# Six instead of four groups a layer by Strassen's scheme, with the differences' buffers moved and one product 512 wide

## The chip, the cores and the metric

The kernel runs on one core of a Trainium2 chip. The metric is the device time of one execution in microseconds. Before the change it is 1974.23 us, the median of three runs (1973.96 to 1975.21). TensorE (PE) multiplies, VectorE (DVE), ScalarE (ACT) and GpSimd (POOL) do the elementwise work, SyncE (SP) issues the transfers of weights.

## The reference, cut to what matters

```python
D_MODEL, SEQ, DEPTH = 2048, 256, 2
D_FF = 5632

def swiglu_ffn(x, g, w_in, w_out):
    h = rms_norm(x, g)
    gate, up = jnp.split(h @ w_in, 2, axis=-1)
    return x + (jax.nn.silu(gate) * up) @ w_out

def reference(...):
    for layer in range(DEPTH):
        if layer < N_REC:                      # layer 0: recurrent block (RG-LRU)
            x = recurrent_block(x, ...)
        else:                                  # layer 1: windowed attention with sinks
            ...
            x = attn_block(x, ..., k_band, v_band)
        x = swiglu_ffn(x, norm2_g[layer], ffn_w_in[layer], ffn_w_out[layer])
    return x
```

All of it is float32. The change touches the product `h @ w_in` of the two FFNs: 256 tokens, 2048 features in, 2 x 5632 out.

## The kernel before

**Tiles and passes.** The activations are kept transposed, features on partitions, 256 tokens (`T`) along the row. A weight chunk is a 128 x 1024 tile: 256 features in (two k tiles) by 512 out. It comes by one transfer into one of four `raw` tiles and is split into a high part (`hi`, on ACT, L306) and the rest (`lo`, on DVE, L309), both in a reduced float type that PE takes in one pass. An activation tile is split in the same way into a slot, 256 columns high, 256 low. A product is then three passes: high by high, high by low, low by high. In an ordinary chunk the weights are the stationary operand (in the ring `hi`/`lo`) and the activations move (in a slot): 2 k tiles x 4 blocks of outputs x 3 = 24 passes of 256 columns, all recorded at L375. Where a block has a whole bank of PSUM, the pair high by (high, low) can be one pass of 512 columns; `RUNS` and `SYNC` put three of these in a row at some places. Groups that are `paired` have two banks for four blocks and use none of them.

**Groups.** 512 columns of `w_in` by all 2048 features is a group: 8 chunks, 192 passes. An FFN has 22. In `ffn` the first `NS` of them go by Strassen's scheme: a chunk is a 2 x 2 product of blocks, done with seven products instead of eight, 21 passes a chunk, which is here called a turn (L476). In a turn the activations are the stationary operand (in slots, or sums of them, `forms`, also in slots) and 256 columns of weights move: either the ring's (`b<-hi,s`, `b<-lo,s`) or differences of the chunk's blocks (`b<-s,s`). The differences are computed by POOL from `raw` (L279 to L281, in `sums`) two sets in turn, and split by ACT (L289) and DVE (L291, in `split_sums`) into slots that `sums` takes from the same pool as all others. At a group's end `fast` adds the four banks into two slots `U` and `V` on DVE; four transposes on PE (L383, L386) turn the finished product back.

**Order.** All chunks are one list, `jobs`. `ffn` puts `AHEAD` = 8 ordinary chunks, then each turn followed by `OWN` = 2 ordinary chunks, then the remaining ordinary ones, then the groups of `w_out` (`project`). `stream` loads a chunk four jobs ahead, splits it three ahead and its differences two ahead. Everything else (norms, gates, split of hidden features: `later`) are background tasks that `run_bg` puts between, as far as a running estimate of DVE and ACT work allows. A task that finds no free slot or bank is asked again later; `need` runs tasks at once where a product must have their result.

**Slots and where they lie.** Slots are tiles of 2 KB a partition, `s0` to `s57`, and are made at their first use, after the other tiles. Tiles are placed in the order in which they are made. The `x`, `raw`, `hi` and `lo` tiles start 96 bytes past a multiple of 128 bytes; two tiles `rstd` of 1032 bytes shift what is made after them, so that all 58 slots start at 32 past such a multiple.

Of the kernel before, what the change touches and what calls it, by code (L numbers as in the profile page):

```python
# [12 lines left out]
F32 = mybir.dt.float32  # L13
F32R = mybir.dt.float32r
# [3 lines left out]
P = 128  # L18
# [31 lines left out]
class Trunk:  # L50
# [15 lines left out]
    DVE_TICK = 640.0  # L66
    ACT_TICK = 800.0

    NS = 4
    AHEAD = 8  # L70
    OWN = 2
    LS = 2
# [2 lines left out]
    def __init__(self, ctx, tc, dram):  # L75
        self.tc, self.nc, self.d = tc, tc.nc, dram
        nc = self.nc
        const = ctx.enter_context(tc.tile_pool(name="const", bufs=1))
        psum = ctx.enter_context(tc.tile_pool(name="psum", bufs=1, space=bass.MemoryType.PSUM))
        tmp = ctx.enter_context(tc.tile_pool(name="tmp", bufs=1))  # L80
        self.tmp = tmp
        self.par = const.tile([P, NPAR], F32, name="par")
        self.con = const.tile([P, NCON], F32, name="con")
        self.cc = const.tile([P, 32], F32, name="cc")
        self.x = [const.tile([P, 4, T], F32, name=f"x{i}") for i in range(4)]
        self.slots = deque(range(58))
        self.spool = const
        self.held = {}
        self.raw = [const.tile([P, 1024], F32, name=f"raw{i}") for i in range(4)]
        self.hi = [const.tile([P, 1024], F32R, name=f"hi{i}") for i in range(4)]  # L90
        self.lo = [const.tile([P, 1024], F32R, name=f"lo{i}") for i in range(4)]
        self.banks = deque(psum.tile([P, 512], F32, name=f"b{i}") for i in range(8))
        self.misc = 0
        self.started = False
        self.xin = 0
        self.other = None
        self.summing = False
        self.opening = None
# [12 lines left out]
        self.dve = 0.0  # L111
        self.act = 0.0
# [34 lines left out]
        self.nc.vector.reciprocal(out, a)  # L147


    def slot(self, dt=F32R):  # L150
        i = self.slots.popleft()
        s = self.spool.tile([P, 2 * T], dt, tag=f"s{i}", name=f"s{i}")
        self.held[id(s)] = (i, s)
        return s

    def free(self, s):
        self.slots.append(self.held.pop(id(s))[0])

    def half(self):
        if self.halves:  # L160
            return self.halves.popleft()
        s = self.slot(F32)
        h = s[:, 0:T]
        self.held[id(h)] = (s, h)
        return h
# [103 lines left out]
    def sums(self, i):  # L269

        raw, tt = self.raw[i % 4], self.nc.gpsimd.tensor_tensor
        if not self.sets:
            self.sets = deque([self.slot(F32), self.slot(F32)] + [self.slot() for _ in range(4)] for _ in range(2))
        s = self.sets.popleft()
        self.sets.append(s)
        self.jobs[i][2]["set"] = s
        b = raw[:, :].rearrange("p (b t) -> p b t", b=4)
        two = lambda q: q.rearrange("p (b t) -> p b t", b=2)
        tt(two(s[0][:, :]), b[:, 0:3:2, :], b[:, 1::-1, :], ALU.subtract)  # L279
        tt(s[1][:, 0:T], raw[:, 2 * T:3 * T], s[0][:, 0:T], ALU.subtract)  # L280
        tt(s[1][:, T:2 * T], raw[:, 3 * T:4 * T], s[1][:, 0:T], ALU.subtract)  # L281

    def split_sums(self, i):

        if len(self.jobs[i]) > 2:
            s = self.jobs[i][2]["set"]
            for z, a, b in ((s[0], s[2], s[3]), (s[1], s[4], s[5])):
                with self.tc.issue_after(self.behind[0]):
                    self.nc.scalar.activation(a, z, AF.Copy)  # L289
                with self.tc.issue_after(self.behind[1]):  # L290
                    self.nc.vector.tensor_tensor(b, z, a.bitcast(F32), ALU.subtract)  # L291
            self.dve += 1400
            self.act += 1200
# [152 lines left out]
    def strassen(self, src, xs, forms, done, last, left):  # L446

        st = {}
        jobs = []
        for c in range(ND // 2):  # L450
            part = {}

            def mm(hi, lo, c=c, part=part):
                if c == 0:
                    st["ps"] = [self.bank() for _ in range(4)]
                    st["begun"] = set()
                ps = st["ps"]
# [6 lines left out]
                t1, t3, t2, t4 = (tuple(s[n + q][:, h * T:h * T + T] for q in (0, 1)) for n in (2, 4) for h in range(2))  # L464
                todo = [(0, 0, A(0, 0), B(1)), (1, 1, A(1, 0), B(3)), (1, 0, S(1), t2), (2, 0, S(0), t1),
                        (2, 1, S(2), t3), (3, 0, S(3), B(2)), (3, 1, A(1, 1), t4)]
                if 0 < c < ND // 2 - 1:
                    todo = [todo[q] for q in (0, 1, 5, 3, 4, 2, 6)]
                if self.other is not None:
                    self.runs = self.RUNS  # L470
                    self.other = None
                for n, (b, h, w, m) in enumerate(todo):
                    if n == 4:
                        self.half_tick()
                    for i, j in ((0, 0), (0, 1), (1, 0)):
                        self.nc.tensor.matmul(ps[b][:, h * T:h * T + T], w[i], m[j], start=b not in st["begun"],  # L476
                                              stop=c == ND // 2 - 1 and i == 1, skip_group_check=True)
                        st["begun"].add(b)
                        self.since += 1
                left[0] -= 1  # L480
                if last and c == ND // 2 - 1:
                    for q in self.sets:
                        for t in q:
                            self.free(t)
                    self.sets = None
                if last:
                    for q in (fh, fl):
                        self.free(q)
                if c == ND // 2 - 1:
                    done(ps)  # L490
            jobs.append((src(c), mm, part))
        return jobs
# [64 lines left out]

    def prep_tile(self, k, gains):

        self.gained(k, gains)  # L560
        yield
        yield from self.squares(k)
# [91 lines left out]
    def ffn(self, l, xs, forms, r, gains, rn, out=None):  # L654
# [6 lines left out]
        def later(g, s):  # L661
            while left[0]:
                yield 1
            for h in range(2):
                while len(self.slots) < 2:
                    yield 1
                q = self.slot()
                self.split_act(q, s[:, h * T:h * T + T])
                hid[2 * g + h].ap = q
                hid[2 * g + h].ready = True  # L670
                yield
            self.free(s)

        for g in range(self.NS):
            def fast(ps, g=g):
                c1, U, V = self.t(), self.slot(F32), self.slot(F32)
                two = lambda q: q.rearrange("p (b t) -> p b t", b=2)
                twice = lambda q: q.unsqueeze(1).broadcast_to([P, 2, T])
                self.a(c1, ps[0][:, 0:T])
                self.tt(two(U[:, :]), two(ps[1][:, :]), twice(c1[:, :]), ALU.add)  # L680
                self.tt(two(V[:, :]), two(ps[2][:, :]), twice(U[:, 0:T]), ALU.add)
                self.tt(U[:, 0:T], ps[2][:, 0:T], V[:, T:2 * T], ALU.add)
                self.tt(V, ps[3], V, ALU.add)
                for b in ps:
                    self.free_bank(b)

                def task():
# [26 lines left out]
        for g in range(self.NS, NH // 2):  # L714
            def done(ps, g=g):
# [4 lines left out]
                def task():  # L720
# [3 lines left out]
                    for h in range(2):  # L724
# [648 lines left out]
```

## Time and profile before

| | |
|---|---|
| median of the runs | 1974.23 us |
| the profiled execution | 1976.51 us, of which the span is 1974.7 us |
| granted TensorE clock | 1.00 |
| Strassen stage, layer 0 | 317 to 568 us |
| Strassen stage, layer 1 | 1278 to 1529 us |
| PE's waits for other engines, in all | 4.9 us |

The span is what the instructions take, from the first to the last. A mean duration of one pass (282 ns for L375) holds its latency; passes overlap, and what counts is the distance from start to start. The chain in order of time gives it: a piece's length divided by its passes.

### The profile page before, as it was taken

The numbers are of one execution on the slowest core, as the hardware profiler recorded it, in microseconds if no ns is written. First come the engines' busy times: TensorE is split into PE (matmuls) and PEld (weight loads), VectorE is DVE, ScalarE is ACT, GpSimd is POOL, SyncE is SP. The second block draws the span as 40 slices with busy tenths as digits, with TensorE's granted clock in tenths as the row PEclk, the third lists the DMA queues.
The fourth block names the chain that finished last, engine by engine and source line by source line (L and its number), as shares of the span: only waits on it lengthen the run. The fifth ranks groups of instructions, "written<-read, shape, count | busy, mean of one in ns | idle before, by whom it ended". The sixth has DMA issues, their size and how long they took to land.

```text
span 1974.7 us, 40978 instructions
## 1 busy us (share of the span) xinstructions
PE 1966.7 (100%) x16762; PEld 1934.6 (98%) x16762; DVE 1428.8 (72%) x2073; ACT 1121.2 (57%) x1746; POOL 383.4 (19%) x356
## 2 busy tenths in 40 slices
PE   9999999999999999999999999999999999999999
PEld 9999999999999999999999889999999999999999
DVE  8988978988986655545668767888889665554443
ACT  6798766555555444434556776655556554444442
POOL 0000125555520000000002454354444000000000
PEclk9999999999999999999999999999999999999999
DMA  8555665665555555555555434565555656556664
GB/s 276 187 190 177 200 209 193 187 208 197 192 201 191 195 193 192 193 193 196 195 185 182 129 129 152 191 214 193 193 193 201 194 193 193 194 196 205 206 205 127
DMA packets 106204, 377.16 MB, mean 191 GB/s; under 512 B 11936, under 2 KB 14368, under 8 KB 106016
## 3 DMA queue, kind: packets, MB, share of 16 engines
q1 hardware_dynamic: 105408, 373.88, 57.7%
q8 instruction: 131, 2.15, 0.4%
q10 hardware_dynamic: 608, 0.66, 0.1%
q14 instruction: 57, 0.47, 0.1%
HBM read 371.88 MB, written 2.10 MB: 189 GB/s over the span
## 4 chain that ended last, share of the span: by engine, by line
PE 96%; DVE 2%; ACT 1%; issue 0%; POOL 0%; DMA 0%; ACTq 0%; DVEq 0%; POOLq 0%
PE b L375 84%; PE b L476 8%; PE b L386 1%; PE b L866 1%; PE b L383 1%; ACT s L123 1%; DVE lo L309 1%; PE b L1052 1%; ACT hi L306 0%; DVE s L1120 0%; DVE s L132 0%; DMA x<-in_x 0%; PE b L1061 0%; PE b L1062 0%; PE b L1063 0%
## 5 line engine op out<-in xcount | busy, mean ns | idle before, releaser
L375 PE MATMUL b<-s,hi 128*128 128x256 f32 (+1 forms) x9536 | 1301.0, 282 | 1.6 <-ACT s L123 1.0
L375 PEld LDWEIGHTS b<-s,hi 128*128 128x128 f32 x9536 | 1203.1, 188 | 21.4 <-ACT s L123 1.7
L309 DVE TENSOR_TENSOR lo<-raw,hi 128x1024 fp32r<-128x1024 f32 (+1 forms) x643 | 812.5, 1266 | 447.4 <-ACT hi L306 444.8
L306 ACT ACTIVATE hi<-raw 128x1024 fp32r<-128x1024 f32 (+1 forms) x643 | 676.0, 1054 | 588.6 <-PE b L375 508.1
L375 PE MATMUL b<-s,lo 128*128 128x256 f32 x4992 | 748.3, 277 | 0.0
L375 PEld LDWEIGHTS b<-s,lo 128*128 128x128 f32 x4992 | 651.0, 188 | 0.5
L279 POOL TENSOR_TENSOR s<-raw 128x512 f32<-128x512 f32 x64 | 120.8, 1888 | 233.3 <-DMA raw<-in_ffn_in 185.6
L291 DVE TENSOR_TENSOR s<-s,s 128x512 fp32r<-128x512 f32 x128 | 141.5, 1141 | 0.6 <-ACT s L289 0.3
L1142 POOL TENSOR_TENSOR s<-s 128x128 f32<-128x128 f32 x32 | 14.7, 462 | 537.0 <-ACT s L123 534.3
L476 PE MATMUL b<-s,s 128*128 128x256 f32 x768 | 105.6, 282 | 0.5 <-DVE s L291 0.5
L299 ACT ACTIVATE hi<-raw 128x768 fp32r<-128x768 f32 x64 | 54.1, 845 | 78.8 <-PE b L375 56.5
L476 PEld LDWEIGHTS b<-s,s 128*128 128x128 f32 x768 | 97.3, 189 | 0.8 <-DVE s L291 0.7
L123 ACT ACTIVATE s<-s 128x256 fp32r<-128x256 f32 (+3 forms) x180 | 69.1, 429 | 33.4 <-POOL s L508 19.5
L132 DVE TENSOR_TENSOR s<-s,s 128x256 fp32r<-128x256 f32 (+3 forms) x148 | 70.6, 509 | 19.8 <-ACT s L123 19.7
L476 PE MATMUL b<-hi,s 128*128 128x256 f32 x384 | 80.7, 281 | 0.0
L280 POOL TENSOR_TENSOR s<-raw,s 128x256 f32<-128x256 f32 x64 | 78.7, 1230 | 5.0
L300 DVE TENSOR_TENSOR lo<-raw,hi 128x768 fp32r<-128x768 f32 x64 | 70.5, 1102 | 12.6 <-PE b L375 8.1
L289 ACT ACTIVATE s<-s 128x512 fp32r<-128x512 f32 x128 | 73.6, 617 | 7.8 <-POOL s L281 7.8
L506 POOL TENSOR_TENSOR s<-s 128x128 f32<-128x128 f32 x16 | 14.0, 877 | 328.8 <-ACT s L123 328.8
L281 POOL TENSOR_TENSOR s<-raw,s 128x256 f32<-128x256 f32 x64 | 70.9, 1108 | 5.0
L476 PEld LDWEIGHTS b<-hi,s 128*128 128x128 f32 x384 | 64.6, 189 | 0.0
L123 ACT ACTIVATE s<-x,par 128x256 fp32r<-128x256 f32 (+1 forms) x112 | 52.6, 498 | 19.9 <-DVE x L132 13.5
(121 smaller groups left out, 1127.4 us busy)
## 6 DMA issues: line engine op xcount, KB each, us to landing
raw<-in_ffn_in SPq DMA_DIRECT2D x352, 512.0 KB, 3.5
raw<-in_ffn_out SPq DMA_DIRECT2D x176, 512.0 KB, 3.4
raw<-in_lru_in SPq DMA_DIRECT2D x62, 512.0 KB, 3.6
raw<-in_lru_out SPq DMA_DIRECT2D x32, 512.0 KB, 3.8
raw<-in_w_q SPq DMA_DIRECT2D x32, 512.0 KB, 3.4
raw<-in_w_o SPq DMA_DIRECT2D x32, 512.0 KB, 3.3
raw<-in_gate SPq DMA_DIRECT2D x8, 512.0 KB, 3.7
raw<-in_kv SPq DMA_DIRECT2D x8, 512.0 KB, 3.4
```

What stands on the lines that cost most here:

```text
L123: self.nc.scalar.activation(out, in_, func, **kw)
L132: self.nc.vector.tensor_tensor(out, a, b, op)
L279: tt(two(s[0][:, :]), b[:, 0:3:2, :], b[:, 1::-1, :], ALU.subtract)
L280: tt(s[1][:, 0:T], raw[:, 2 * T:3 * T], s[0][:, 0:T], ALU.subtract)
L281: tt(s[1][:, T:2 * T], raw[:, 3 * T:4 * T], s[1][:, 0:T], ALU.subtract)
L289: self.nc.scalar.activation(a, z, AF.Copy)
L291: self.nc.vector.tensor_tensor(b, z, a.bitcast(F32), ALU.subtract)
L300: low = self.nc.vector.tensor_tensor(lo[:, q], raw[:, q], hi[:, q].bitcast(F32), ALU.subtract)
L306: high = self.ins(self.nc.scalar.activation(hi[:, q], raw[:, q], AF.Copy))
L309: low = self.nc.vector.tensor_tensor(lo[:, q], raw[:, q], hi[:, q].bitcast(F32), ALU.subtract)
L375: self.nc.tensor.matmul(*args, **kw)
L476: self.nc.tensor.matmul(ps[b][:, h * T:h * T + T], w[i], m[j], start=b not in st["begun"], stop=c == ND // 2 - 1 and i == 1, skip_group_ch ...
```

## The change

`NS` is 6 instead of 4. Of the slots, `s57` to `s64` are now made right behind `lo`, ahead of the `rstd` tiles, and form a pool of their own (`odd`); `sums` puts the split differences there, and other F32 slots use it when it is free. The second pair of differences is split in two halves, so that high and low part of one difference stand side by side in a slot. The turn starts with the product of the fourth difference: its high by (high, low) is one pass of 512 columns into a whole bank (L484), and the low by high another; the other six products share the other three banks. `fast` adds the additional half bank. The scratch for dynamic DMAs is cut from its 16 KB to 2 KB a partition, where the additional slots go. Some tasks wait for more free slots.

```diff
-    NS = 4
+    NS = 6
...
-        self.slots = deque(range(58))
+        self.slots = deque(range(57))
+        self.odd = deque(range(57, 65))
...
+        for i in self.odd:
+            self.spool.tile([P, 2 * T], F32R, tag=f"s{i}", name=f"s{i}")
...
-    def slot(self, dt=F32R):
-        i = self.slots.popleft()
+    def slot(self, dt=F32R, odd=None):
+        odd = bool(self.odd) and dt == F32 if odd is None else odd
+        i = (self.odd if odd else self.slots).popleft()
...
-            self.sets = deque([self.slot(F32), self.slot(F32)] + [self.slot() for _ in range(4)] for _ in range(2))
+            self.sets = deque([self.slot(F32, False) for _ in range(2)] + [self.slot(F32R, True) for _ in range(4)]
+                              for _ in range(2))
...
-            for z, a, b in ((s[0], s[2], s[3]), (s[1], s[4], s[5])):
+            for z, a, b in ((s[0], s[2], s[3]), (s[1][:, 0:T], s[4][:, 0:T], s[4][:, T:2 * T]),
+                            (s[1][:, T:2 * T], s[5][:, 0:T], s[5][:, T:2 * T])):
...
-                todo = [(0, 0, A(0, 0), B(1)), (1, 1, A(1, 0), B(3)), (1, 0, S(1), t2), (2, 0, S(0), t1),
-                        (2, 1, S(2), t3), (3, 0, S(3), B(2)), (3, 1, A(1, 1), t4)]
+                t1, t3 = (tuple(s[2 + q][:, h * T:h * T + T] for q in (0, 1)) for h in range(2))
+                t2, t4 = (tuple(q[:, h * T:h * T + T] for h in range(2)) for q in s[4:6])
+                todo = [(0, 0, A(1, 1), t4), (3, 1, A(0, 0), B(1)), (1, 0, S(1), t2), (1, 1, A(1, 0), B(3)),
+                        (2, 0, S(0), t1), (2, 1, S(2), t3), (3, 0, S(3), B(2))]
                 if 0 < c < ND // 2 - 1:
-                    todo = [todo[q] for q in (0, 1, 5, 3, 4, 2, 6)]
+                    todo = [todo[q] for q in (0, 1, 3, 6, 4, 5, 2)]
...
-                    for i, j in ((0, 0), (0, 1), (1, 0)):
+                    if n == 0:
+                        self.nc.tensor.matmul(ps[b], w[0], s[5], start=b not in st["begun"],
+                                              stop=c == ND // 2 - 1, skip_group_check=True)
+                        st["begun"].add(b)
+                    for i, j in ((0, 0), (0, 1), (1, 0))[2 * (n == 0):]:
...
@@ prep_tile @@
+        while len(self.slots) < 3:
+            yield 1
...
@@ later @@
-                while len(self.slots) < 2:
+                while len(self.slots) < 4:
...
-                self.a(c1, ps[0][:, 0:T])
+                self.a(c1, ps[3][:, T:2 * T])
...
-                self.tt(V, ps[3], V, ALU.add)
+                self.tt(V[:, 0:T], ps[3][:, 0:T], V[:, 0:T], ALU.add)
+                self.tt(V[:, T:2 * T], ps[0][:, 0:T], V[:, T:2 * T], ALU.add)
+                self.tt(V[:, T:2 * T], V[:, T:2 * T], c4, ALU.add)
...
-                        if both is not None or h == 0 and left[0]:
+                        if both is not None or h == 0 and (left[0] or len(self.slots) < 8):
...
-    nc = bacc.Bacc("TRN2", target_bir_lowering=False, num_devices=1)
+    nc = bacc.Bacc("TRN2", target_bir_lowering=False, num_devices=1, dynamic_dma_scratch_size=2048)
```

Two places show how the instructions stand. The first is PE in a turn in the middle of a group of layer 0; a row is line, operation, output, moving operand, stationary operand and size. Before, from the third product on; `s44` and `s45` are differences, `s34` and `s51` a chunk's forms:

```order
L476 MATMUL b5_88<-hi2_77,s34_3334 128x256
L476 MATMUL b5_88<-lo2_81,s34_3334 128x256
L476 MATMUL b5_88<-hi2_77,s51_3335 128x256
L476 MATMUL b4_87<-s44_3869,s34_3334 128x256
L476 MATMUL b4_87<-s45_3870,s34_3334 128x256
L476 MATMUL b4_87<-s44_3869,s51_3335 128x256
```

After, from the head of the turn; `s57`, `s59` and `s60` are differences, `s33` and `s32` activations, `s1` and `s49` forms:

```order
L484 MATMUL b2_93<-s60_3880,s33_3233 128x512
L488 MATMUL b2_93<-s60_3880,s33_3233 128x256
L488 MATMUL b5_96<-hi2_77,s32_3219 128x256
L488 MATMUL b5_96<-lo2_81,s32_3219 128x256
L488 MATMUL b5_96<-hi2_77,s32_3219 128x256
L488 MATMUL b3_94<-hi2_77,s33_3233 128x256
L488 MATMUL b3_94<-lo2_81,s33_3233 128x256
L488 MATMUL b3_94<-hi2_77,s33_3233 128x256
L488 MATMUL b5_96<-hi2_77,s1_3342 128x256
L488 MATMUL b5_96<-lo2_81,s1_3342 128x256
L488 MATMUL b5_96<-hi2_77,s49_3343 128x256
L488 MATMUL b4_95<-s57_3877,s1_3342 128x256
```

The product of a difference that closed the turn now opens it, with a pass of 512 columns, and the differences come from slots 57 and up.

The second place is DVE at the end of the first Strassen group of layer 0, where the ring's splits (L309 and L300), the splits of differences (L291) and the group's sums (L132, from banks `b`) stand in one queue. Before:

```order
L291 TENSOR_TENSOR s57_3876<-s52_3873,s31_3875 128x512
L291 TENSOR_TENSOR s40_3878<-s53_3874,s55_3877 128x512
L309 TENSOR_TENSOR lo3_82<-raw3_74,hi3_78 128x1024
L300 TENSOR_TENSOR lo0_79<-raw0_71,hi0_75 128x768
L132 TENSOR_TENSOR s56_4643<-b3_86,t1_92 128x512
L132 TENSOR_TENSOR s35_4644<-b4_87,s56_4643 128x512
L132 TENSOR_TENSOR s56_4643<-b4_87,s35_4644 128x256
L132 TENSOR_TENSOR s35_4644<-b5_88,s35_4644 128x512
```

After (L316 and L307 are the ring's splits, L298 those of differences, L135 the sums):

```order
L135 TENSOR_TENSOR s45_4659<-b3_94,t1_100 128x512
L135 TENSOR_TENSOR s46_4660<-b4_95,s45_4659 128x512
L316 TENSOR_TENSOR lo1_80<-raw1_72,hi1_76 128x1024
L135 TENSOR_TENSOR s45_4659<-b4_95,s46_4660 128x256
L135 TENSOR_TENSOR s46_4660<-b5_96,s46_4660 128x256
L135 TENSOR_TENSOR s46_4660<-b2_93,s46_4660 128x256
L298 TENSOR_TENSOR s59_3878<-s15_3875,s57_3877 128x512
L135 TENSOR_TENSOR s46_4660<-s46_4660,t2_101 128x256
L298 TENSOR_TENSOR s58_3879<-s19_3876,s58_3879 128x256
L298 TENSOR_TENSOR s60_3880<-s19_3876,s60_3880 128x256
```

The sums are six instead of four, with a ring split and a split of differences between them, and a set of differences is split by three instructions instead of two.

More of the change, by code (lines that the diff above doesn't have):

```diff
@@ L156, in free @@
     def free(self, s):
-        self.slots.append(self.held.pop(id(s))[0])
+        i = self.held.pop(id(s))[0]
+        (self.slots if i < 57 else self.odd).append(i)
     def half(self):
@@ L161, in half @@
             return self.halves.popleft()
-        s = self.slot(F32)
+        s = self.slot(F32, False)
         h = s[:, 0:T]
@@ L463, in mm @@
                 s = part["set"]
-                t1, t3, t2, t4 = (tuple(s[n + q][:, h * T:h * T + T] for q in (0, 1)) for n in (2, 4) for h in range(2))
-                todo = [(0, 0, A(0, 0), B(1)), (1, 1, A(1, 0), B(3)), (1, 0, S(1), t2), (2, 0, S(0), t1),
-                        (2, 1, S(2), t3), (3, 0, S(3), B(2)), (3, 1, A(1, 1), t4)]
+                t1, t3 = (tuple(s[2 + q][:, h * T:h * T + T] for q in (0, 1)) for h in range(2))
+                t2, t4 = (tuple(q[:, h * T:h * T + T] for h in range(2)) for q in s[4:6])
+                todo = [(0, 0, A(1, 1), t4), (3, 1, A(0, 0), B(1)), (1, 0, S(1), t2), (1, 1, A(1, 0), B(3)),
+                        (2, 0, S(0), t1), (2, 1, S(2), t3), (3, 0, S(3), B(2))]
                 if 0 < c < ND // 2 - 1:
-                    todo = [todo[q] for q in (0, 1, 5, 3, 4, 2, 6)]
+                    todo = [todo[q] for q in (0, 1, 3, 6, 4, 5, 2)]
                 if self.other is not None:
@@ L675, in fast @@
             def fast(ps, g=g):
-                c1, U, V = self.t(), self.slot(F32), self.slot(F32)
+                c1, c4, U, V = self.t(), self.t(), self.slot(F32), self.slot(F32)
                 two = lambda q: q.rearrange("p (b t) -> p b t", b=2)
                 twice = lambda q: q.unsqueeze(1).broadcast_to([P, 2, T])
-                self.a(c1, ps[0][:, 0:T])
+                self.a(c1, ps[3][:, T:2 * T])
                 self.tt(two(U[:, :]), two(ps[1][:, :]), twice(c1[:, :]), ALU.add)
                 self.tt(two(V[:, :]), two(ps[2][:, :]), twice(U[:, 0:T]), ALU.add)
+                self.a(c4, ps[0][:, T:2 * T])
                 self.tt(U[:, 0:T], ps[2][:, 0:T], V[:, T:2 * T], ALU.add)
-                self.tt(V, ps[3], V, ALU.add)
-                for b in ps:
+                self.tt(V[:, 0:T], ps[3][:, 0:T], V[:, 0:T], ALU.add)
+                self.tt(V[:, T:2 * T], ps[0][:, 0:T], V[:, T:2 * T], ALU.add)
+                self.tt(V[:, T:2 * T], V[:, T:2 * T], c4, ALU.add)
+                for b in (ps[1], ps[2], ps[3], ps[0]):
                     self.free_bank(b)
@@ L730, in task @@
                         yield
-                        if both is not None or h == 0 and left[0]:
+                        if both is not None or h == 0 and (left[0] or len(self.slots) < 8):
+                            while h == 0 and not (self.slots or self.odd):
+                                yield 1
                             if h == 0:
```

## The prediction

> **What bounds the kernel now.** I read the page's totals, the chain that ended last and PE's own waits first; then the chain piece by piece in the Strassen stage, because the change replaces work there; then the same view where two kinds of pass alternate without anything else between; then the stage's busy times for what has to stay hidden.
>
> ```profile
> span 1974.7 us, 40978 instructions
> PE 1966.7 (100%) x16762; PEld 1934.6 (98%) x16762; DVE 1428.8 (72%) x2073; ACT 1121.2 (57%) x1746; POOL 383.4 (19%) x356
> PE 96%; DVE 2%; ACT 1%; issue 0%; POOL 0%; DMA 0%; ACTq 0%; DVEq 0%; POOLq 0%
> PE b L375 84%; PE b L476 8%; PE b L386 1%; PE b L866 1%; PE b L383 1%; ACT s L123 1%; DVE lo L309 1%; PE b L1052 1%; ACT hi L306 0%; DVE s L1120 0%; DVE s L132 0%; DMA x<-in_x 0%; PE b L1061 0%; PE b L1062 0%; PE b L1063 0%
> ```
>
> PE has work all the time. So the time is a count of passes times the distance between their starts, and both move here. In PE's own list of waits (below, the longest) nothing is worth removing.
>
> ```profile
> PE b L383 <- ACT h L123: 1.2, 1, 1.2
> ```
>
> The stage of layer 0, chain in order of time (start us, us, line, passes):
>
> ```profile
> 375.38 5.65 PE b L375 x48
> 381.03 2.46 PE b L476 x21
> 383.49 4.24 PE b L375 x36
> 387.73 0.11 PE b L383
> 387.84 0.33 PE b L386 x3
> 388.17 1.42 PE b L375 x12
> 389.59 2.46 PE b L476 x21
> 392.04 5.44 PE b L375 x48
> 397.48 2.49 PE b L476 x21
> ```
>
> Two ordinary chunks (48 passes) take 5.44 us, 113.3 ns a pass, or 5.65 us, 117.7 ns. Same work, same operands: PE has a short and a long pace, and each lasts until something else runs. A Strassen turn of 21 passes takes 2.46 to 2.49 us, 117 to 119 ns a pass, whatever the pace around it. The two last chunks between groups (375.38, and 383.49 with 388.17) go at the long pace, the six others of a group at the short one.
>
> The stage of keys and values alternates 12 ordinary passes (L1052: weight from the ring `hi`/`lo`, moving operand from a slot) with 12 turned ones (L1061 to L1063: weight from a slot, moving from the ring):
>
> ```profile
> 1009.91 1.36 PE b L1052 x12
> 1011.28 0.12 PE b L1061
> ...
> 1012.69 1.41 PE b L1052 x12
> 1014.11 0.12 PE b L1061
> ...
> 1015.48 0.57 PE b L1052 x5
> ```
>
> Short ordinary is followed by long turned (1011.28 to 1012.69, 1.41), that by long ordinary (1.41), that by short turned (1014.11 to 1015.48, 1.37, 114 ns) and that by short ordinary again. So turned passes can be as short as ordinary ones; going from ordinary to turned flips the pace, going back keeps it. Passes with both operands in slots are never short. Twelve of them that start at 365.85 take 1.44 us up to 367.29, 120 ns each:
>
> ```profile
> 365.85 1.59 PE L476 MATMUL b<-s,s 128*128 128x256 f32 x12
> 367.29 0.39 PE L375 MATMUL b<-s,hi 128*128 128x256 f32 x2
> ```
>
> **Passes.** Four more groups (two a layer) go from ordinary to Strassen. Each leaves 8 x 24 = 192 ordinary passes: 768 x 113.3 ns = -87.0 us. Strassen turns go from 64 to 96. The old ones cost 64 x 2.485 = 159.0 us (most are 2.49; the page's 8% of the span says 158). The new turn is one product 512 wide and 19 of 256, and with the differences in slots 57 to 64, which start at the ring's offset within 128 bytes (96, against 32 for the other slots, from the sizes of the tiles made ahead of them), every pass of it is of the turned kind; none has both operands in the other slots. The order of the turn on PE, shown with the change, has it so: `s44`, `s45`, `s21`, `s23` gave the differences before, `s57` to `s64` do now, and the product that stood at the end leads, with two of its passes in one.
>
> What a 512 wide pass of this kind costs and does to the pace, the trace of before does not show. The nearest are three in a row in an ordinary chunk, with long passes ahead and short ones behind:
>
> ```profile
> 46.45 1.10 PE L375 MATMUL b<-s,lo 128*128 128x256 f32 x8
> 47.39 1.10 PE L375 MATMUL b<-s,hi 128*128 128x256 f32 x5
> 48.33 0.62 PE L375 MATMUL b<-s,lo 128*128 128x256 f32 x4
> 48.78 0.39 PE L375 MATMUL b<-s,hi 128*128 128x256 f32 x2
> ```
>
> Ahead: 0.94 us for 8 (117 ns); behind: 0.45 for 4 (113). The five between hold two of 256 and three of 512: (0.94 - 2 x 0.1175) / 3 = 0.235 us. The other end is two short passes, 0.227. I take 0.23; over 96 turns the ends differ by 0.8 us. So a pass of 512 saves nothing by itself, but three in a row can turn long into short. I take it that one at the head of a turn does this too: the flip from ordinary to turned is undone, the turn is short, and it hands the short pace back. Then a turn is 0.23 + 12 passes in 1.37 + 7 at 0.1133 = 2.39 us, and 96 make 229.4: against 159.0, +70.4 us.
>
> **Long chunks behind turns.** Two in eight turns now hand over the long pace: 16 of 64 pairs, at 5.65 - 5.44 = 0.21, is 3.4 us. With short turns at every place in the group they go: -3.4 us. If they stay at the same share, it is 24 pairs, +1.7 instead. Threes of 512 wide products in ordinary chunks get rarer, since more groups are of the narrow kind; as priced above they cost what their halves cost, and it is left at nothing.
>
> **Transposes.** Each Strassen group is turned back by four transposes, 0.11 + 0.33 = 0.44 us above: four groups, +1.8 us.
>
> **DVE, ACT, POOL.** These are hidden, and the cover is thin on DVE:
>
> ```profile
> 317.00:568.00 251.00, 251.00 (x2174) 250.95 (x2174) 229.00 (x249) 143.30 (x208) 133.66 (x91) 1.00 0.60 196
> 568.00:1009.00 441.00, 441.00 (x3765) 435.93 (x3764) 254.15 (x323) 208.66 (x268) 0.00 (x0) 1.00 0.59 195
> L309 DVE TENSOR_TENSOR lo<-raw,hi 128x1024 fp32r<-128x1024 f32 x64 | 91.6, 1431 | 14.1 <-ACT hi L306 14.1
> L291 DVE TENSOR_TENSOR s<-s,s 128x512 fp32r<-128x512 f32 x63 | 72.2, 1180 | 0.5 <-ACT s L289 0.3
> L132 DVE TENSOR_TENSOR s<-s,s 128x256 fp32r<-128x256 f32 x22 | 10.9, 539 | 0.0
> L132 DVE TENSOR_TENSOR s<-b,s 128x512 f32<-128x512 f32 x6 | 4.2, 692 | 0.6
> L132 DVE TENSOR_TENSOR s<-b,s 128x256 f32<-128x256 f32 x3 | 1.3, 424 | 0.1
> ```
>
> DVE is busy 229.0 of 251.0 us, 7.16 of each 7.84 us turn with its two chunks. One of two splits becomes two halves: 2 x 539 - 1180 gives -0.1 us a turn, the spread of 128x512 and 128x256 rows at most +0.15. The sums of a group (the second place shown with the change) go from 3 x 692 + 424 = 2.5 to 2 x 692 + 4 x 424 = 3.1 us a group, 0.07 a turn. DVE then needs 7.1 to 7.4 of a 5.44 + 2.39 = 7.83 us turn: still hidden, at up to 94%. Behind it wait the ring's `lo` tiles, for which PE would stand; the ring is split three jobs ahead, about 8 us, which covers a burst. POOL and ACT do the same work per turn, in half of it. The stage grows by 16 turns a layer and the rest of the FFN shrinks, so held-back splits of hidden features are done nearer to `ffn_out`. I allow 1 us for lateness there, between 0 and 4. The waits for free slots that are added stand in these background tasks and can only push the same work later; the weight transfers on SP stay the same in number and order, and POOL's sums come per turn as before.
>
> The smaller DMA scratch I cost at nothing: the page's queues that carry weights are all hardware ones:
>
> ```profile
> q1 hardware_dynamic: 105408, 373.88, 57.7%
> ```
>
> The Trainium skill ("SBUF — State Buffer", SBUF size) calls that scratch the ring of descriptors that GpSimd writes; by that rule too the cut is free, as no queue here is of that kind.
>
> Sum: -87.0 + 70.4 - 3.4 + 1.8 + 1.0 = -17.2 us. It is made against an execution that took 1976.51 us, 2.3 above the median of 1974.23; taken off the median: 1957.0 us.
>
> **Rivals.** (b) One 512 wide pass does not touch the pace. Then ordinary and turned alternate as in the stage of keys and values: half the turns are long, 0.235 + 19 x 0.1175 = 2.47, and half the pairs between, 48 x 0.21 = 10.1 us. With 48 x 0.08 = 3.8 more in the turns that is 13.9 back: 1970.9. For it: that stage; against: the three in a row above.
> (c) The pass of 512 leaves the long pace each time, and the way back keeps it, as at 1012.69. Then all 96 turns lose 0.08 and all 96 pairs 0.21: +27.8, which ends at 1984.8, slower than before. It decides from 17.2 / 0.29 = 59 turns of 96. Against it: the short passes at 48.33.
> (d) Placement is nothing to PE, the long pace is that of the Strassen products themselves: turns stay near 0.235 + 19 x 0.1186 = 2.49, +9.6, and long pairs at their share, +5.1: 1971.7. Against it: the short L1061 rows. The Trainium skill ("TensorE: Matmul & The Clock Gate", Step-by-step) has it that loading the next weights takes no read bandwidth from the running matmul, by which placement could not matter. The trace disagrees: the turned passes at 1014.11 and those of two slots at 365.85 differ by 5% with equal shapes.
> (e) DVE becomes the bound of the stage: it would have to reach 7.83 us a turn, 0.4 over my highest; each 0.1 beyond costs 9.6 us. At 8.0, 17 us, no gain is left: about 1974. Two-input DVE work is slowed beside POOL (1431 ns in the stage's L309 row against a mean of 1266 over the kernel), and the stage is half longer.
>
> ```profile
> L309 DVE TENSOR_TENSOR lo<-raw,hi 128x1024 fp32r<-128x1024 f32 (+1 forms) x643 | 812.5, 1266 | 447.4 <-ACT hi L306 444.8
> ```
>
> **How the numbers follow.** My forecast (a) 0.58, (b) 0.17, (c) 0.06, (d) 0.11, (e) 0.08. (a) by itself spans 1953 to 1962: with passes at 113.3 throughout a turn nears 2.38, with no lateness it gains 2 more, with lateness of 4 and some long pairs it loses 5. The range goes up to 1972 to take in (b) and (d): 1953 to 1972. A change of 0.2%, about 4 us, is what a measurement of this kernel can tell from none: faster is below 1970.3. That holds for (a), for about half of (b) and (d), which lie at the line, and part of (e): 0.76 faster, 0.15 the same, 0.09 slower.
>
> **What would show it.** Right: turns of 20 passes in 2.38 to 2.40 us and pairs of chunks at 5.44 nearly throughout the chain; PE's waits still of a few us; 88% to 94% DVE in the stage. Rows of 5.65 at every other pair say (b), at all pairs (c), turns of 2.47 to 2.49 between short pairs (d), and PE waiting for DVE `lo` or split rows (e). I am wrong above all if a single 512 wide pass does not do what three did.

## The result: 1.3% slower, and the profile after

The changed kernel takes 2000.39 us (median of four runs, 1995.74 to 2003.27) against 1974.55 (four runs, 1973.96 to 1975.21): ratio 1.0129, 95% interval 1.0108 to 1.0149. Forecast were 1957.0 and a range of 1953 to 1972. The profiled execution took 2003.27 us. Its page has, for the lines shown of before (span, busy times, the chain that ended last by engine):

```profile
span 2001.5 us, 41409 instructions
PE 1965.8 (98%) x16691; PEld 1928.1 (96%) x16691; DVE 1524.0 (76%) x2233; ACT 1152.0 (58%) x1902; POOL 505.6 (25%) x452
PE 84%; DVE 9%; ACT 5%; issue 2%; POOL 1%; DMA 0%; ACTq 0%; DVEq 0%; POOLq 0%
```

PE has fewer passes, as was counted on (16691 for 16762), yet the span is 26.8 us longer and PE is no longer busy all of it: DVE and ACT now hold 14% of the chain, against 3%. PE's own waits, the two longest (total us, times, longest), and below them the only wait for such a split in the profile of before:

```profile
PE b L484 <- DVE s L298: 25.0, 25, 1.8
PE b L390 <- POOL s L1205: 4.6, 4, 2.6
```

```profile
PE b L476 <- DVE s L291: 0.5, 1, 0.5
```

The product that opens a turn (L484) waits in 25 of 96 turns for the split of a difference (L298); before, one pass of 64 turns did. The chain in order of time shows where (start, length, line, passes):

```profile
349.91 0.23 PE b L484
350.14 2.15 PE b L488 x19
352.30 4.95 PE b L382 x44
357.25 0.89 DVE s L298
358.14 0.04 issue
358.18 0.50 PE b L484
358.68 2.24 PE b L488 x19
360.92 5.65 PE b L382 x48
366.58 0.23 PE b L484
366.81 2.17 PE b L488 x19
...
378.66 1.97 DVE lo L316
380.63 1.00 DVE s L135 x3
381.63 0.10 DVE s L298
...
382.93 0.68 DVE s L298 x2
383.61 0.04 issue
383.65 0.50 PE b L484
```

An undisturbed turn is what was forecast: 0.23 + 2.15 to 2.17 = 2.38 to 2.40 us, with pairs of 5.44 between (from the one at 352.30 the chain goes over to DVE's split, which ends later). At 358.18 a late turn stands: its head, 0.50 in the chain for 0.23 and 0.34 from its start to the next pass's start, then a turn and a pair at the long pace (2.24, 5.65), and the next head restores the short one. At 383.65, the first turn of the second group, the split stands behind that group end's ring split and sums, as the rows of DVE's order shown with the change have it; two passes of the turn's ring product run ahead of the head there. With PE's starts taken one after the other, the distance ahead of the heads holds 29 us more than that of plain passes: 16.7 at all 12 first turns of a group, 8.4 at ten sixth ones, 4.1 at three third ones.

What DVE and POOL do ahead of 358 (timeline: start, length, engine, line, operation):

```profile
353.44 1.22 DVE L316 TENSOR_TENSOR lo<-raw,hi 128x1024 fp32r<-128x1024 f32 x1
354.58 3.55 DVE L298 TENSOR_TENSOR s<-s,s 128x512 fp32r<-128x512 f32 x3
354.08 1.75 POOL L285 TENSOR_TENSOR s<-raw 128x512 f32<-128x512 f32 x1 [5.08 <-DMA raw<-in_ffn_in]
...
357.05 0.80 POOL L287 TENSOR_TENSOR s<-raw,s 128x256 f32<-128x256 f32 x1
```

The three splits of a set take 3.55 us while POOL forms the next set beside them, and the fourth difference, which the head needs, is split last. DVE as a whole has time left: 352.86 us of 392 in the stage (the row is shown with the experiment that decides).

### The profile page after: what moved, and what is told of

Same layout as the page of the kernel before. It is cut to its first block, busy times and chain, and to the rows that moved or that the text cites. A ratio compares the mean times of both kernels' runs of the same rounds, so it can differ in the third digit from the quotient of the medians.

```text
span 2001.5 us, 41409 instructions
## 1 busy us (share of the span) xinstructions
PE 1965.8 (98%) x16691; PEld 1928.1 (96%) x16691; DVE 1524.0 (76%) x2233; ACT 1152.0 (58%) x1902; POOL 505.6 (25%) x452
## 4 chain that ended last, share of the span: by engine, by line
PE 84%; DVE 9%; ACT 5%; issue 2%; POOL 1%; DMA 0%; ACTq 0%; DVEq 0%; POOLq 0%
PE b L382 70%; PE b L488 10%; DVE lo L316 3%; ACT s L126 2%; DVE s L298 2%; DVE s L135 2%; ACT hi L313 1%; PE b L484 1%; DVE s L1139 1%; ACT L126 1%; PE b L393 1%; PE b L1071 1%; PE b L390 0%; DVE s L139 0%; DVE h L135 0%
## 5 line engine op out<-in xcount | busy, mean ns | idle before, releaser
L382 PE MATMUL b<-s,hi 128*128 128x256 f32 (+1 forms) x9128 | 1234.9, 281 | 1.0 <-DVE h L135 0.6
L382 PEld LDWEIGHTS b<-s,hi 128*128 128x128 f32 x9128 | 1145.9, 188 | 16.5 <-ACT s L126 1.1
L316 DVE TENSOR_TENSOR lo<-raw,hi 128x1024 fp32r<-128x1024 f32 (+1 forms) x611 | 776.4, 1273 | 357.4 <-ACT hi L313 355.0
L382 PE MATMUL b<-s,lo 128*128 128x256 f32 x4736 | 709.3, 277 | 0.1
L285 POOL TENSOR_TENSOR s<-raw 128x512 f32<-128x512 f32 x96 | 192.4, 2004 | 388.4 <-DMA raw<-in_ffn_in 307.0
L298 DVE TENSOR_TENSOR s<-s,s 128x256 fp32r<-128x256 f32 (+1 forms) x288 | 244.5, 898 | 0.0
L488 PE MATMUL b<-s,s 128*128 128x256 f32 x960 | 145.3, 278 | 0.0
L488 PE MATMUL b<-hi,s 128*128 128x256 f32 x576 | 123.3, 278 | 0.0
L296 ACT ACTIVATE s<-s 128x256 fp32r<-128x256 f32 (+1 forms) x288 | 118.3, 474 | 1.1 <-POOL s L287 1.1
L307 DVE TENSOR_TENSOR lo<-raw,hi 128x768 fp32r<-128x768 f32 x96 | 109.4, 1140 | 11.8 <-ACT hi L306 6.4
L286 POOL TENSOR_TENSOR s<-raw,s 128x256 f32<-128x256 f32 x96 | 108.4, 1129 | 7.5
L135 DVE TENSOR_TENSOR s<-s,s 128x256 fp32r<-128x256 f32 (+3 forms) x184 | 84.7, 490 | 23.9 <-ACT s L126 23.6
L287 POOL TENSOR_TENSOR s<-raw,s 128x256 f32<-128x256 f32 x96 | 91.5, 953 | 7.5
L488 PE MATMUL b<-lo,s 128*128 128x256 f32 x288 | 80.0, 278 | 0.0
```

The costliest lines, as they stand in the source:

```text
L135: self.nc.vector.tensor_tensor(out, a, b, op)
L307: low = self.nc.vector.tensor_tensor(lo[:, q], raw[:, q], hi[:, q].bitcast(F32), ALU.subtract)
L316: low = self.nc.vector.tensor_tensor(lo[:, q], raw[:, q], hi[:, q].bitcast(F32), ALU.subtract)
L382: self.nc.tensor.matmul(*args, **kw)
```

## The experiments

Times are medians, and a ratio is to the kernel before on the same chip, whose median lay between 1974.55 and 1976.38 us; a difference of two kernels that ran on different chips is uncertain by that much. Line numbers move by one where an edit adds a line. Three theories stand against each other throughout: (1) deadline, the moved product reads a split that is issued last and has too little time to it; (2) capacity, DVE has too much work in the stage, in whatever order; (3) pace, the pass of 512 or the placement doesn't do what was counted on.

**Split the fourth difference first** (`t4first`).

```diff
-            for z, a, b in ((s[0], s[2], s[3]), (s[1][:, 0:T], ...), (s[1][:, T:2 * T], ...)):
+            for z, a, b in ((s[1][:, T:2 * T], ...), (s[0], s[2], s[3]), (s[1][:, 0:T], ...)):
```

> The changed kernel with one edit: of a chunk's three splits of differences, that of the fourth difference is issued first instead of last. Theory 1 (deadline: the turn now opens with the difference whose split is issued last, so PE waits for that split though DVE has time on average): PE's wait for DVE at the 512 wide product falls from 25.0 us to under 10, the time to 1965 to 1985. Theory 2 (capacity: six groups need more DVE work in the stage than fits): the order of three splits does not matter, 1995 to 2003. Theory 3 (the two paces of PE: long turns and long pairs are the loss): no change either, about 2000.

Measured: 1979.35 us, ratio 1.0025 (1.0015 to 1.0034). 21 of the 26 us come back by the order of three instructions. That is inside theory 1's range; theories 2 and 3 had no change. What is left is the same wait, at the head and at later products of the turn:

```profile
PE b L484 <- DVE s L298: 4.2, 7, 1.5
PE b L488 <- DVE s L298: 4.2, 12, 0.7
```

**Close the turn with the fourth difference, its pass of 512 included** (`t4last`).

```diff
+                todo = todo[1:] + todo[:1]
-                    if n == 0:
+                    if n == 6:
...
-                    for i, j in ((0, 0), (0, 1), (1, 0))[2 * (n == 0):]:
+                    for i, j in ((0, 0), (0, 1), (1, 0))[2 * (n == 6):]:
```

> The changed kernel with one edit: the product of the fourth difference, with its 512 wide pass, closes the turn instead of opening it. Theory 1 (deadline): the split gets some 18 passes, 2 us, more; PE's wait for DVE splits falls under 6 us and the time to 1955 to 1968 (the lower end if a 512 wide pass undoes the flip of the pace at the end of a turn too, the upper if turns are then long, 2.47). Theory 2 (capacity): waits only move to another product, 1990 to 2003. Theory 3 (pace): if the place of the 512 wide pass sets the pace, turns of 2.47 and long pairs behind: 2000 or more.

Measured: 1986.19 us, ratio 1.0057 (1.0042 to 1.0072). The time lies between the ranges of theories 1 and 3. PE's waits for the splits, and the busy times in layer 0's stage (PE, PEld, DVE, ACT, POOL, with counts):

```profile
PE b L489 <- DVE s L298: 1.1, 3, 0.6
PE b L485 <- DVE s L298: 0.7, 2, 0.4
317.00:701.10 384.10, 383.39 (x3221) 380.32 (x3220) 343.05 (x429) 221.98 (x366) 205.22 (x138) 1.00 0.58 194
```

The waits fall from 25.0 to 1.8 us, though DVE is nearly as busy as in the changed kernel (343.05 of 384.10 us, 89%; there 352.86 of 392, 90%, the row stands with `ls3`) and its splits are as long (1108 ns for 128x512 and 781 for 128x256; 1080 and 808 there). So the place of the product takes the waits away, and theory 2 falls. But the chain reads:

```profile
404.51 2.05 PE b L489 x18
406.56 0.23 PE b L485
406.79 0.12 PE b L489
406.90 5.66 PE b L382 x48
```

Every pair is long; by distances of starts, 2249 of the 2256 ordinary passes in layer 0's stage and 2236 in layer 1's. The turns stay short (2.05 + 0.23 + 0.12 = 2.40), so this is the half of rival (c) that concerns the pairs, at its price: about 94 x 0.21 = 20 us. Where the 512 wide pass stands decides which pace it leaves.

**Four groups again, all else as changed** (`ns4`): `NS = 6` to `NS = 4`.

> The changed kernel with four groups a layer again, placement, 512 wide pass and order of the turn kept. Theory 1 (deadline): 8 groups keep their waits, two thirds of 25 us plus their long turns, against shorter turns (64 x 0.1 = 6.4) and fewer long pairs (3.4): 1980 to 1992. Theory 2 (capacity): DVE has the room it had before, no waits: 1962 to 1968. Theory 3 (pace): in between, by the share of long turns: 1970 to 1985.

Measured: 1998.44 us, ratio 1.0111 (1.0096 to 1.0126), with 16.9 us of waits at the head, 18 times, in 64 turns. The waits are two thirds of 25.0, as theory 1 had them, so the loss is in each group's turns, not in their number; the time is 6 us over theory 1's range.

**Six groups and the smaller scratch, turns as before** (`before_ns6`): in the kernel before, `NS = 6`, 65 slots in one pool, the scratch of 2048.

> The kernel before with six groups a layer and 65 slots in one pool (scratch of dynamic DMAs at 2 KB to make room); old order of the turn, old placement, no 512 wide pass. Theory 1 (deadline): no waits, 768 passes out (-87.0), 32 turns of 2.485 in (+79.5), transposes +1.8, long pairs +1.7: 1970 (1968 to 1974). Theory 2 (capacity): DVE is too slow for six groups, PE waits as in the changed kernel: 1990 to 2003. Theory 3 (pace): as theory 1.

Measured: 1976.62 us, ratio 1.0004 (0.9995 to 1.0013). The median turn is the old 2.49, PE waits 0.9 us for splits, not the tens of us that theory 2 asks for, and the time is 3 us over theory 1's range. In the profiled executions, 0.9 us apart in their spans, the gain goes so: four groups more save 87.0 us of passes and cost 32 x 2.49 = 79.7 and 1.8 of transposes, and of the remaining 5.5 PE's wait for POOL between the stages takes 2.7 (3.0 us for 0.3) and more long ordinary passes 1.3 (9.8 us for 8.5, by starts). The scratch costs nothing that shows.

**Open with a product that needs no difference** (`ring512`). Each `hi` and `lo` become two halves of one tile `hl`, so that a pass of 512 can read both; the turn opens with a ring product and closes with the fourth difference; a set has two splits again, and a group's sums are five (six in the changed kernel, four before).

```diff
+        self.hl = [const.tile([P, 2048], F32R, name=f"hl{i}") for i in range(4)]
-                todo = [(0, 0, A(1, 1), t4), (3, 1, A(0, 0), B(1)), ...]
+                todo = [(0, 0, A(0, 0), B(1)), (1, 1, A(1, 0), B(3)), ..., (3, 1, A(1, 1), t4)]
-                        self.nc.tensor.matmul(ps[b], w[0], s[5], ...)
+                        self.nc.tensor.matmul(ps[b]..., w[0], pair, ...)
```

> Six groups, differences placed as in the changed kernel, but the turn opens with a product of the ring: each pair of ring tiles is one tile, so that one pass of 512 columns takes high and low of a ring block. The fourth difference closes the turn again, differences are split by two instructions as before, and a group's sums are five instead of six. Theory 1 (two conditions: every difference stands ready in time, and a 512 wide pass opens the turn): no waits, turns of 2.38, pairs at 5.44: 1954 to 1962. Theory 2 (DVE has too little room for six groups): PE still waits for DVE, 1970 to 1995. Theory 3 (placement and the 512 wide pass bring nothing): as the kernel before with six groups, 1974 to 1978.

Measured: 1966.66 us, ratio 0.9958 (0.9946 to 0.9971): faster than the kernel before and the changed one, but 5 us over theory 1's range. The only wait of its turns in PE's list (total us, times, longest) is

```profile
PE b L489 <- DVE s L298: 2.9, 7, 0.8
```

The edit takes work off DVE too (a set's splits take 2 x 1096 ns here, 1080 + 2 x 808 in the changed kernel, and a group has one sum less), so it does not show by itself that the place of the first reader does it; `t4last`, with DVE nearly as busy as in the changed kernel, does.

**The same with two passes of 256 at the head** (`ring256`). The product at the head needs half a bank then, and a group's sums are four.

```diff
-                    if n == 0:
-                        self.nc.tensor.matmul(ps[b]..., w[0], pair, ...)
-                    for i, j in ((0, 0), (0, 1), (1, 0))[2 * (n == 0):]:
+                    for i, j in ((0, 0), (0, 1), (1, 0)):
```

> As ring512, with the 512 wide pass as two of 256 and the kernel before's four sums. Theory 1: without the 512 wide pass the pace flips at each way into a turn, so half of the turns are long (2.47) and half of the pairs (5.65): 10 to 14 us over ring512. Theory 3: the same as ring512 within 2 us.

Measured: 1975.73 us, ratio 1.0006 (0.9997 to 1.0015). Long and short alternate exactly as rival (b) described, with 1112 and 1104 of 2256 ordinary passes long in the two stages:

```profile
430.81 5.65 PE b L383 x48
436.47 2.40 PE b L485 x21
438.86 5.44 PE b L383 x48
444.31 2.48 PE b L485 x21
```

One pass of 512 at the head is worth 9 us here, a little under the 10 to 14 expected, and rival (b), by which such a pass does nothing, is refuted.

**Four groups with that turn** (`ring512_ns4`): `NS = 4` in `ring512`.

> As ring512, with four groups a layer. Theory 1: against the kernel before, 64 turns shorter by 0.1 (6.4) and long pairs gone (3.4): 1963 to 1967, so two more groups a layer are worth 6 to 9 us. Theory 2 (DVE has too little room for six): this one is faster than ring512. Theory 3: 1972 to 1976.

Measured: 1971.64 us, ratio 0.9983 (0.9974 to 0.9992). That is 5 us over theory 1's range. Two more groups a layer are worth 5.0 us with the short turn (1966.66), where 6 to 9 were expected, and nothing with the old one.

**Another alignment, same offsets from each other** (`pad_before`): in the kernel before, `par` gets eight more columns, by which ring and slots start at 0 and 64 instead of 96 and 32 past a multiple of 128.

> The kernel before with its first tile 32 bytes longer, so that the ring starts at a multiple of 128 bytes and the slots 64 past one; nothing else. If the offset of an operand within 64 bytes costs each pass something, a short pass gets nearer to the 106.7 ns that 256 columns take at the 213.3 ns per 512 columns: up to 6% off, 1860 to 1950. If only the offset of ring against slots matters: the same as before within 2 us.

Measured: 1974.45 us, ratio 0.9998 (0.9989 to 1.0007). Moved together by 32 bytes the operands cost the same; what placement does (below, `ring512_place`) appears when some are moved against the others. What in that place matters was not tried further.

**Splits one job earlier** (`ls3`), the changed kernel with one number changed; PE's passes stand in the same order.

```diff
-    LS = 2
+    LS = 3
```

> The changed kernel with the splits of a difference taken one job earlier (LS = 3 for 2); PE's own order of passes is unchanged, and the program puts at least 36 passes (4 us) between a split and the first pass that reads it, where the changed kernel has 4 at its closest. Theory 1 (deadline: the moved product reads the split issued last): the waits of the 512-wide pass for the split, 25.0 + 13.9 us in the trace, fall under 5, and with them the long pace that follows a wait; turns 2.38, pairs 5.44, and 1956 to 1967 us. Theory 2 (capacity: DVE has too much to do in the stage, whatever the order): the waits stay over 25 us and move to the group sums; 1990 to 2003 us. Theory 3 (pace: the 512-wide pass at the head doesn't hold the short pace unless PE has waited): waits gone but over half of the ordinary passes at 117.7 ns; 1968 to 1978 us.

Measured: 1964.96 us, ratio 0.9948 (0.9934 to 0.9961). One number takes back 35 us. (The 13.9 us in the expectation are the weight loads of the same heads, that is the same waits a second time.) The engines' busy times, PE's longest wait, and the same stretch of the chain:

```profile
PE 1949.7 (99%) x16691; PEld 1917.2 (98%) x16691; DVE 1473.4 (75%) x2233; ACT 1154.6 (59%) x1902; POOL 527.2 (27%) x452
PE b L484 <- DVE s L298: 3.3, 3, 1.7
380.16 0.23 PE b L484
380.39 2.16 PE b L488 x19
382.55 2.73 PE b L382 x24
385.27 0.11 PE b L390
385.38 0.33 PE b L393 x3
385.71 2.83 PE b L382 x24
```

The first turn of a group no longer waits: the same 2233 instructions of DVE are on time. Busy times in layer 0's stage (PE, PEld, DVE, ACT, POOL, with counts), of the changed kernel and of this one:

```profile
317.00:709.00 392.00, 380.97 (x3236) 376.50 (x3237) 352.86 (x433) 221.94 (x366) 189.03 (x138) 1.00 0.59 191
```

```profile
316.30:692.60 376.30, 374.45 (x3238) 372.00 (x3237) 325.96 (x431) 222.25 (x365) 199.78 (x139) 1.00 0.61 198
```

DVE is even busy 27 us less, so this run alone does not tell whether the earlier splits or the shorter work took the waits away; that the place of the first reader is enough is shown by `t4last`. A job earlier the splits of differences run before POOL's next set, not beside it, and what POOL now runs beside are the ring's splits, which have time. The timeline there:

```profile
352.38 1.36 DVE L298 TENSOR_TENSOR s<-s,s 128x512 fp32r<-128x512 f32 x3
353.66 4.01 DVE L316 TENSOR_TENSOR lo<-raw,hi 128x1024 fp32r<-128x1024 f32 x2
353.38 1.52 POOL L285 TENSOR_TENSOR s<-raw 128x512 f32<-128x512 f32 x1 [3.43 <-DMA raw<-in_ffn_in]
```

**The control** (`before_ls3`): `LS = 3` in the kernel before. It asks whether earlier splits, or the shorter DVE work that comes with them, are worth something in a kernel whose PE does not wait for splits.

> The control: the kernel before with splits one job earlier (LS = 3 for 2) and nothing else. Theory 1 (deadline): there the closest first use lies 17 passes, 1.9 us, behind its split and most of them 42 to 51, and PE waits for a split once, 0.5 us; so the edit that takes 35 us from the changed kernel takes at most 3 here: 1971 to 1976 us. Rival: an earlier split is better in any Strassen stage, whatever the place of the product that needs it (DVE's sums and the ring's splits come in a better order), so that the same edit brings two thirds of it for two thirds of the groups: 1950 to 1960 us.

Measured: 1973.84 us, ratio 0.9992 (0.9983 to 1.0001). DVE's splits got shorter here too (72.2 us of the stage before, shown in the prediction):

```profile
L291 DVE TENSOR_TENSOR s<-s,s 128x512 fp32r<-128x512 f32 x62 | 49.6, 830 | 4.5 <-ACT s L289 3.9
```

and PE gained nothing by it. The edit that is worth 35 us with the moved product is worth about 1 without it.

**Both repairs** (`ring512_ls3`): `LS = 3` in `ring512`.

> The kernel whose turn opens with the 512-wide ring product, with splits one job earlier (LS = 3). Theory 1: what is left of lateness there, about 6 us at the ends of the groups, is a split behind the sums too, so 1959 to 1964 us, against 1966.7 without. Theory 2: DVE is behind by its sums, not by the place of the splits, so within 1.5 us of 1966.7.

Measured: 1961.07 us (1958.73 to 1961.48), ratio 0.9925 (0.9913 to 0.9938), the fastest of all. No turn waits for a difference; the longest wait left is the attention block's for POOL, 4.4 us in three times.

**Placement undone** (`ring512_place`): in `ring512`, slots 57 to 64 are made behind the `rstd` tiles again.

> The kernel whose turn opens with the 512-wide ring product, with the split differences of the odd slots placed behind the other tiles again, where the kernel before has them (slots 57 to 64 of the pool). Rival (d) of the prediction: if the placement of the differences does nothing, within 1.5 us of 1966.7. If it does what the prediction counted on (a turned pass at 113.3 ns against 117.7 or more): 96 turns of 19 passes by 4.4 ns give 8 us more, or half of it when half of the operands are moved; 1970 to 1976 us, with turns of 2.43 to 2.48 in place of 2.38.

Measured: 1972.65 us, ratio 0.9984 (0.9975 to 0.9993), 6 us more than `ring512` by the medians, 4 when each is taken against the kernel before on its own chip. The turns are longer and pairs are now and then long:

```profile
436.05 0.23 PE b L485
436.28 2.22 PE b L489 x19
438.50 5.65 PE b L383 x48
```

The median turn is 2.45 us against 2.385, by starts. It is the passes that read a moved slot that got longer: those with a difference as the moving operand have a median of 119 ns (113 in `ring512`), those with the ring keep 113. Rival (d) is refuted: placement matters, though it is a little over half of the way from the old 2.49.

## Why the prediction was wrong, point by point

PE's time is added up here from the start of each pass to the start of the next, by kind, in the profiled executions, as a difference to the kernel before (160.3 us in turns, 1717.9 in ordinary passes, 91.9 in transposes and all else):

| term | forecast | changed | `ls3` | `ring512_ls3` |
|---|---|---|---|---|
| turns | +70.4 | +88.7 | +69.6 | +68.8 |
| ordinary passes: fewer -87.0, long pairs -3.4, lateness +1.0 | -89.4 | -63.8 | -83.1 | -86.1 |
| transposes and the rest | +1.8 | +1.8 | +1.3 | +0.8 |
| sum | -17.2 | +26.8 | -12.2 | -16.5 |

**Right.** The passes, the transposes and the turn. 2.39 was forecast for the turn; its median is 2.40 with the late ones in it, and 2.385 in the kernels that aren't late. That the 512 wide pass at the head hands back the short pace and that placement shortens the turn is shown by undoing each (`ring256`, `ring512_place`). So the mechanism that the change was costed on exists, and in `ring512_ls3` the sum comes out within 1 us of it (-16.5 against -17.2). That it is so near is partly luck: this kernel opens its turn with another product, and its rows miss the forecast's by 1.6, 3.3 and 1.0 in opposite directions. One reading was too strong: passes with both operands in slots were said to be never short; by starts 32 of the 768 in the turns of before are (112 to 114 ns), the median is 120.

**The step that failed** is the cover by DVE: "still hidden, at up to 94%". It put PE's waits for the splits of differences at nothing, because DVE needs 7.1 to 7.4 of a 7.83 us turn, and a share says nothing about a deadline. The runs showed 29 us of such waits. (The 1.0 us in the sum, "I allow 1 us for lateness there, between 0 and 4", was for the splits of hidden features near `ffn_out`; PE's list of waits has none of that kind that grew.) Of all readers of a difference one lost much of its time: the fourth difference is split last of its set, its product stood last in the turn, and moving it to the head took the 18 passes ahead of it, 2 us, off its time. By the written order of the program the closest first use of a split is 17 passes behind it before, 4 passes after, and 36 in `ls3`. The prediction pointed at both halves of this, the order of the turn on PE and the group's sums on DVE, and didn't lay them side by side. In its costs it asked who waits behind DVE only for the ring's `lo`.

**What the waits cost.** Of the 44 us by which the profiled execution misses the forecast, the waits ahead of the heads are 29.3, less the 1.0 allowed elsewhere. (13.5 of them stand in the row of turns, since in ten first turns of a group two passes of the turn go ahead of its head; the others stand in the row of ordinary passes.) A late turn is also longer in itself, by its head (0.34 from start to start for 0.23) and the long pace behind it: without the waits the turns take 4.5 us more than at the mean of those that were on time (2.41). A wait also flips the pace of the pair that follows, so the long ordinary passes did not go (11.1 us over the short pace, before 8.5, forecast 3.4 less): 6. The attention block's wait for POOL (L1205) grew by 4.3. That is 43.1; the rest is spread.

**The rivals.** (b), (c) and (d) are refuted for this turn; of (c) the long pairs hold for the turn that closes with the wide pass. (e) named the right engine, and its sign, PE waiting for split rows, is what came, but its mechanism was wrong: it had DVE reach 7.83 us a turn, and DVE needed 352.86 / 48 = 7.35 us a turn, inside the forecast's 7.1 to 7.4, when PE stood. With DVE as the bound, another place of one product (`t4last`) would not have taken the waits away. (e) was to decide only 0.4 us over the highest estimate of DVE's work, which made the slower side look far off; what decided was the 2 us that the moved product lost.

**Not settled.** `ls3` keeps 4 us over `ring512_ls3`: three late heads of 3.3 us in all explain most of it. How much of the 35 us of `ls3` is due to the earlier splits and how much to DVE's shorter work was not separated. Why a wait, or a pass of 512, changes the pace is not shown, nor by what means placement acts: no run shows that a weight load takes read bandwidth from a running pass. Why POOL is later for the attention block in the kernels with six groups or the new turn (1.9 to 4.6 us for 0.3) was not tried.

## What to carry to other kernels

When a consumer is moved earlier, write down for each of its inputs the instruction that makes it, that instruction's place in its own queue, and the time from there to the first use before and after; an engine's share of busy time can't answer for it. A cover of "90% busy" hides work on average and hides nothing at the point where a burst (a group's sums) meets the item that is made last. When a reordering loses, try the look-ahead before giving up the reordering: here one number was worth 35 us, more than the change itself was to bring.

## What was not expected of the hardware

The pace of PE's passes (113.3 or 117.7 ns for 256 columns) is flipped by waits as well as by operands, and where a 512 wide pass stands in a turn sets which pace follows: at the head the short one (`ring512`), one pass before the end the long one at nearly every pair (`t4last`, 5.66).

DVE's split of a set took 3.55 us beside POOL's work and 1.36 us ahead of it (the two timelines above); over the 96 sets of the changed kernel it took 1.35 to 3.56. The Trainium skill ("SBUF — State Buffer", Who interferes with whom) says that a DVE instruction with two inputs in SBUF contends with a GpSimd instruction that reads SBUF; these rows agree, and add the size: 2.2 us on the path of a product that had no time for it.
